# Attention scores: the low-part product on 64 rows of TensorE, with two banks in separate row groups

## The chip, the cores and the metric

The kernel runs on one core of one Trainium2 chip. The metric is the device time of one execution in microseconds (us): the median of the runs. One more execution was profiled, and its trace is what the rows below come from.

## The reference, cut to what matters

The reference is one inference step of a two-layer network. Each layer has three branches, and the third is grouped-query attention over 1024 latent tokens plus 128 context tokens. There are 8 query heads of 64 channels and 2 key/value heads, each shared by four query heads:

```python
def one_block(qi):
    sc = jnp.einsum('bqkgd,bskd->bkgqs', qi, k).astype(jnp.float32) * scale
    p = jax.nn.softmax(sc, axis=-1).astype(v.dtype)
    return jnp.einsum('bkgqs,bskd->bqkgd', p, v)
```

For a latent query, `k` has 1152 rows: the 1024 latent keys and the 128 cached ones. A second, small attention of the 128 prompt tokens over themselves runs once per layer. All inputs and outputs are float32. The other branches (a state-space scan, a Fourier mixing) and the projections that merge the three do not change.

## The kernel before

**How precision is kept.** TensorE is fed with float32 values that are split into a high part of few mantissa bits and a low remainder. A product of two values is built from high times high, high times low and low times high. A head has only 64 channels, so for the attention scores the two parts are stacked on the 128 rows of TensorE: the query tile `at_Q` holds the high part of its 64 channels in partitions 0 to 63 and the low part in 64 to 127. The key tile `at_K` has two planes: plane 0 holds the key's high part twice (in partitions 0 to 63 and again in 64 to 127), plane 1 the key's low part twice. A product of all 128 rows with plane 0 gives (high + low of the query) times the key's high part. A product with plane 1 gives (high + low of the query) times the key's low part.

**The scores.** `scores(i)` works on one item, which is one head `h` and one block `s` of 128 queries. There are 64 items per layer, so 128 in all. The 1152 keys are three columns of 384, one in each bank of the PSUM tile `pa`, which has one buffer. Each bank gets two matmuls (planes 0 and 1): six matmuls per item, each with its own weight load of the same 128 x 128 query block.

**What follows an item.** `softmax` finds the row maximum on VectorE (line 1107), takes the exponential with the row sum on ScalarE (line 143), and scales on VectorE (line 1111). `trans` turns the item's nine 128 x 128 blocks on TensorE into `pt` and `pv` banks, from which ScalarE and VectorE write the high and low parts `at_PT`. `pvm` multiplies two items' turned blocks with the values (18 matmuls), and `pv_out` adds the two halves of its result over the tile `at_t`.

**The order of the work.** `step(x)` issues `scores` of item x, then `trans` of item x - 1, then lets one group of twelve matmuls of a projection run beside it (`merges`, the blocks of `dense`), and in every second step `pvm` of the pair before. The framework draws up each engine's list at compile time, mostly in program order with ready work moved ahead, and each engine then runs its list in order. All loads and stores of these stages are issued by SyncE (SP), in one list as well.

**The tiles beside it.** `load_q(h + 1)` brings the next head's 1024 query columns at `s == 2`. The prompt's value tile `at_Vp`, the prompt's scratch `at_t` and the loads `th` of `proj_block(1, ...)`, three buffers deep, take SBUF space in the same pool.

Of the kernel before, what the change touches and what calls it, by code (L numbers as in the profile page):

```python
# [10 lines left out]
R = mybir.dt.float32r  # L11
# [8 lines left out]
SP = 128  # L20
# [5 lines left out]
NH = 8  # L26
# [76 lines left out]
class Program:  # L103
# [1007 lines left out]
        nc.vector.tensor_scalar(P[:, :n], P[:, :n], mx[:, 2:3], None, op0=OP.mult)  # L1111

    def pv_out(self, pv, n, dst):
        t = self.sb("at_t", [64, 256], bufs=1, pool=self.gp)
        self.act(t[:, :n], pv[64:128, :n])
        self.tt(dst, pv[0:64, :n], t[:, :n], OP.add)

    def attn_gen(self, l, qs_d, k_d, v_d, sgc_d, zc_d):
        nc, G = self.nc, self.gp
        KV, Q, Y, PT = {}, {}, {}, {}  # L1120

        def load_k(kv):
            KV["k", kv] = self.sb("at_K", [128, 2, 1152], R, pool=G)
            for a in range(2):
                for c in range(0, 1152, 576):
                    self.dma(KV["k", kv][:, a, c:c + 576], k_d[kv, a, :, 128 + c:704 + c])
                    yield 1

        def load_v(kv):
            KV["v", kv] = self.sb("at_V", [128, 9, 128], R, pool=G)  # L1130
            for c0, c1 in ((0, 5), (5, 9)):
                self.dma(KV["v", kv][:, c0:c1], v_d[kv, :, 1 + c0:1 + c1])
                yield 1

        def load_q(h):
            Q[h] = self.sb("at_Q", [128, SL], R, bufs=2, pool=G)
            for c in (0, 512):
                self.dma(Q[h][:, c:c + 512], qs_d[h, :, SP + c:SP + c + 512])
                yield 1

        def scores(i):
            h, s = i
            K = KV["k", h // 4]
            ps = self.ps.tile([128, 3, 512], F, name="pa", tag="pa", bufs=1)
            for j in range(3):
                for a in range(2):
                    self.mm(ps[:, j, :384], Q[h][:, 128 * s:128 + 128 * s], K[:, a, 384 * j:384 + 384 * j], a == 0, a == 1)
            P = self.sb("at_P", [128, 1152], bufs=2, pool=G)
            self.softmax(ps[:, :, :384], 1152, P)
            return P  # L1150

        def trans(i, P):
            h, s = i
            if s % 2 == 0:
                PT[h, s // 2] = [self.sb(f"at_PT{a}", [128, 9, 256], R, pool=G) for a in range(2)]
            T = PT[h, s // 2]
            c = 128 * (s % 2)
            for b in range(0, 9, 3):
                pt = self.pst("pv" if b == 6 else "pt")
                for k in range(3):  # L1160
                    self.tr(pt[:, 128 * k:128 * k + 128], P[:, 128 * (b + k):128 * (b + k) + 128])
                self.split_ps(T[0][:, b:b + 3, c:c + 128], T[1][:, b:b + 3, c:c + 128], pt[:, :384].rearrange("p (k n) -> p k n", n=128))

        def pvm(h, p):
            T = PT.pop((h, p))
            Vt = KV["v", h // 4]
            pv = self.pst("pv")
            n = 0
            for a in range(2):
                for k in range(9):  # L1170
                    self.mm(pv[:, :256], Vt[:, k], T[a][:, k], n == 0, n == 17)
                    n += 1
            self.pv_out(pv, 256, Y[h // 2][64 * (h % 2):64 * (h % 2) + 64, 256 * p:256 + 256 * p])

        def prompt():
            kp = self.sb("at_Kp", [128, 2, 2, 128], R, pool=G)
            self.dma(kp, k_d[:, :, :, 0:SP].rearrange("k a p n -> p (k a) n"))
            qp = self.sb("at_Q", [128, SL], R, bufs=2, pool=G)
            self.dma(qp.rearrange("p (h n) -> p h n", h=NH), qs_d[:, :, 0:SP].rearrange("h p n -> p h n"))
            vp = self.sb("at_Vp", [128, 2, 128], R, pool=G)  # L1180
            self.dma(vp, v_d[:, :, 0].rearrange("k p c -> p k c"))
            sg = self.sb("at_Yp", [128, 4, 128], bufs=2, pool=G)
            self.dma(sg, sgc_d[:, 0:SP].rearrange("(b p) n -> p b n", p=128))
            yield 5
            k, q = load_k(0), load_q(0)
            yield from self.some(k, 2)
            ps = self.ps.tile([128, 3, 512], F, name="pa", tag="pa", bufs=1)
            for h in range(NH):
                for a in range(2):
                    self.mm(ps[:, h // 4, 128 * (h % 4):128 * (h % 4) + 128], qp[:, 128 * h:128 * h + 128], kp[:, h // 4, a], a == 0, a == 1)  # L1190
            src = ps[:, 0:2].rearrange("p a (h n) -> p (a h) n", n=128)
            mx = self.sb("at_mp", [128, 3, NH], pool=G)
            nc.vector.tensor_reduce(out=mx[:, 0], in_=src, axis=AX.X, op=OP.max, negate=True)
            P = self.sb("at_P", [128, 1152], bufs=2, pool=G)
            P3 = P[:, 0:SL].rearrange("p (h n) -> p h n", n=128)
            for h in range(NH):
                self.act(P3[:, h], src[:, h], AF.Exp, bias=mx[:, 0, h:h + 1], accum=mx[:, 1, h:h + 1])
            nc.vector.reciprocal(mx[:, 2], mx[:, 1])
            self.tt(P3, P3, mx[:, 2][:, :, None].to_broadcast([128, NH, 128]), OP.mult)
            yield from k  # L1200
            yield from q
            yield from step(0)
            v = load_v(0)
            T = [self.sb(f"at_PT{a}", [128, 9, 256], R, pool=G).rearrange("p k n -> p (k n)") for a in range(2)]
            for q in range(2):
                pt = self.pst("pt")
                for k in range(4):
                    self.tr(pt[:, 128 * k:128 * k + 128], P3[:, 4 * q + k])
                c = slice(512 * q, 512 * q + 512)
                self.split_ps(T[0][:, c], T[1][:, c], pt)  # L1210
            yield from v
            y = self.sb("at_Yp", [128, 4, 128], bufs=2, pool=G)
            for q in range(2):
                pv = self.pst("pv")
                for a in range(2):
                    self.mm(pv, vp[:, q], T[a][:, 512 * q:512 * q + 512], a == 0, a == 1)
                for u in range(2):
                    t = self.sb("at_t", [64, 256], bufs=1, pool=G)
                    self.act(t, pv[64:128, 256 * u:256 * u + 256])
                    for e in range(2):  # L1220
                        self.tt(y[64 * e:64 * e + 64, 2 * q + u], pv[0:64, 256 * u + 128 * e:256 * u + 128 * e + 128], t[:, 128 * e:128 * e + 128], OP.add)
            self.tt(y, y, sg, OP.mult)
            self.dma(zc_d[:, 0:SP].rearrange("(b p) n -> p b n", p=128), y)

        def finish(hb):
            y = Y.pop(hb)
            for c0, c1 in ((128, 384), (384, 768), (768, 1152)):
                w = c1 - c0
                sg = self.sb("jt", [128, 384], bufs=3)
                self.dma(sg[:, :w], sgc_d[128 * hb:128 * hb + 128, c0:c1])  # L1230
                z = self.jo()
                self.tt(z[:, :w], y[:, c0 - 128:c1 - 128], sg[:, :w], OP.mult)
                self.dma(zc_d[128 * hb:128 * hb + 128, c0:c1], z[:, :w])

        items = [(h, s) for h in range(NH) for s in range(8)]
        n = len(items)
        Ps = {}

        def step(x):
            if x < n:  # L1240
                h, s = items[x]
                if x == 32:
                    self.run_all(load_k(1))
                if x == 34:
                    self.run_all(load_v(1))
                if s == 2 and h % 2 == 0:
                    Y[h // 2] = self.sb("at_Y", [128, SL], bufs=1, pool=G)
                if s == 2 and h + 1 < NH:
                    self.run_all(load_q(h + 1))
                Ps[x] = scores(items[x])  # L1250
            if 1 <= x <= n:
                trans(items[x - 1], Ps.pop(x - 1))
            yield PACE[x % 2]
            if x >= 2 and x % 2 == 0:
                h, s = items[x - 2]
                pvm(h, s // 2)
                if h % 2 == 1 and s == 6:
                    finish(h // 2)

        yield from prompt()  # L1260
        for x in range(1, n + 1):
            yield from step(x)
# [71 lines left out]
    def layer(self, l, cs):  # L1334
# [65 lines left out]
        def proj_block(n, b, th, key):  # L1400
            def ev(j, ps):
                if n == 1:
                    t = th_tile()
                    self.dma(t, rows(th["d"], b, j))
                else:
                    t = self.jt(rows(th["d"], b, j)) if "d" in th else th.pop(j)
# [256 lines left out]
```

## Time and profile before

| | |
|---|---|
| median of 3 runs | 2709.13 us (2707.88 to 2715.88) |
| the profiled execution's own time | 2707.93 us |
| its span, first to last instruction | 2706.2 us |
| granted TensorE clock, mean over the span | 0.991 of full speed |
| attention of layer 0, from its first to its last scores | about 750 to 1106 us of the span |
| attention of layer 1 | about 2070 to 2425 us |

In the profile PE is TensorE's matmuls and PEld its weight loads, which overlap matmuls. A matmul's length in a row includes its way through the array: the next one can start long before it ends. What the engine really needs per matmul is the distance from one start to the next. A weight load's row also holds more than its share of the engine. Where a matmul has to wait for its weights, the matmul's row begins with the load and is longer than usual, and the next weight load starts when that matmul really begins to stream.

### The profile page before, as it was taken

The page shows a single profiled execution, that of the slowest core. Times are in us where ns is not written, and L with a number is a line of the kernel's source. Part 1 is how long each engine was busy: PE and PEld are TensorE (multiplying, and loading weights), DVE is VectorE, ACT ScalarE, POOL GpSimd, SP SyncE. Part 2 cuts the span into 40 slices and gives each one's busy share as a digit, 9 for nine tenths or more (in the row PEclk, how much of TensorE's full clock was granted, in tenths as well). Part 3 has the DMA queues.
Part 4 walks back from the last instruction along what each step waited for, and adds up shares of the span by engine and source line. Part 5 has one row for each costly group of instructions (what it writes and reads, how often), then busy time and mean ns, then how long its engine had stood idle before and what let it go on. Part 6 is the DMA issues. An engine that isn't in the chain of part 4 may idle for free. (4 is left out here: it accounts for less than half of the span.)

```text
span 2706.2 us, 44496 instructions
## 1 busy us (share of the span) xinstructions
PE 2599.8 (96%) x16093; PEld 2502.1 (92%) x16093; DVE 1746.8 (65%) x3837; ACT 1200.5 (44%) x2754; POOL 655.4 (24%) x518
## 2 busy tenths in 40 slices
PE   6999999999999999999999999989999999999998
PEld 4999999899999899999989999989999998999997
DVE  6559964636478889847462798564654788981443
ACT  5462245741355465423345322575224556543244
POOL 1332122312321020132333312232222212101223
PEclk8999999999999999999999999999999999999999
DMA  7533233566443435535542322345645334442334
GB/s 258 154 103 102 90 105 106 168 185 199 149 139 110 143 118 154 188 96 138 172 134 86 112 86 83 119 131 166 210 142 192 104 116 155 148 125 80 92 117 145
DMA packets 459812, 366.85 MB, mean 136 GB/s; under 512 B 72816, under 2 KB 431816, under 8 KB 459592
## 3 DMA queue, kind: packets, MB, share of 16 engines
q1 hardware_dynamic: 458168, 359.68, 43.4%
q0 software_dynamic: 1424, 4.33, 0.5%
q8 instruction: 127, 2.08, 0.3%
q14 instruction: 93, 0.76, 0.1%
HBM read 243.52 MB, written 120.39 MB: 134 GB/s over the span
## 5 line engine op out<-in xcount | busy, mean ns | idle before, releaser
L169 PE MATMUL pd<-hh,whi 128*128 128x384 f32 x2496 | 854.3, 343 | 8.8 <-ACT jo L143 4.5
L169 PE MATMUL pd<-hh,wlo 128*128 128x384 f32 x2496 | 842.9, 338 | 4.7 <-POOL wlo L146 4.4
L169 PE MATMUL pd<-hl,whi 128*128 128x384 f32 x2496 | 840.2, 337 | 0.8 <-DVE hl L150 0.8
L146 POOL TENSOR_TENSOR wlo<-wst,whi 128x512 fp32r<-128x512 f32 x312 | 432.8, 1389 | 1523.1 <-ACT whi L143 1445.4
L169 PEld LDWEIGHTS pd<-hh,whi 128*128 128x128 f32 x2496 | 470.9, 189 | 14.9 <-ACT jo L143 6.1
L169 PEld LDWEIGHTS pd<-hh,wlo 128*128 128x128 f32 x2496 | 470.8, 189 | 10.0 <-POOL wlo L146 9.0
L169 PEld LDWEIGHTS pd<-hl,whi 128*128 128x128 f32 x2496 | 471.3, 189 | 2.9 <-DVE hl L150 1.9
L169 PE MATMUL pd<-A,whi 128*128 128x384 f32 x1728 | 457.7, 341 | 6.3 <-ACT jo L143 6.3
L143 ACT ACTIVATE whi<-wst 128x512 fp32r<-128x512 f32 x312 | 195.6, 630 | 291.1 <-PE pd L169 188.2
L169 PEld LDWEIGHTS pd<-A,whi 128*128 128x128 f32 x1728 | 310.9, 189 | 9.0 <-ACT jo L143 6.9
L169 PE MATMUL pd<-A,wlo 128*128 128x384 f32 x864 | 293.5, 340 | 0.0
L1107 DVE TENSOR_REDUCE at_mx<-pa 128x1 f32<-128x1152 f32 x128 | 173.2, 1353 | 16.0 <-PE pa L169 15.6
L143 ACT ACTIVATE at_PT<-pt 128x384 fp32r<-128x384 f32 (+1 forms) x260 | 114.9, 490 | 142.6 <-PE pt L174 142.2
L169 PE MATMUL pa<-at_K,at_Q 128*128 128x384 f32 x768 | 167.1, 347 | 7.8 <-ACT at_P L143 5.3
L143 ACT ACTIVATE at_P<-pa,at_mx 128x1152 f32<-128x1152 f32 x128 | 158.0, 1235 | 20.6 <-DVE at_mx L1107 19.4
L169 PEld LDWEIGHTS pd<-A,wlo 128*128 128x128 f32 x864 | 163.2, 189 | 0.1
L169 PEld LDWEIGHTS pa<-at_K,at_Q 128*128 128x128 f32 x768 | 128.2, 188 | 28.2 <-ACT at_P L143 25.2
L169 PE MATMUL pt<-qkW,hh 128*128 128x384 f32 x576 | 151.9, 345 | 0.5 <-DVE qk_xn L146 0.5
L169 PE MATMUL pv<-at_PT,at_V 128*128 128x256 f32 x1152 | 148.8, 283 | 0.0
L143 ACT ACTIVATE jo<-pd 128x384 f32<-128x384 f32 x120 | 58.1, 485 | 199.9 <-PE pd L169 113.0
L169 PEld LDWEIGHTS pv<-at_PT,at_V 128*128 128x128 f32 x1152 | 144.7, 191 | 0.8
L146 DVE TENSOR_TENSOR at_PT<-pt,at_PT 128x384 fp32r<-128x384 f32 (+1 forms) x260 | 133.1, 550 | 9.3 <-ACT at_PT L143 8.6
(297 smaller groups left out, 3719.5 us busy)
## 6 DMA issues: line engine op xcount, KB each, us to landing
aw<-in_ada_w_dram SPq DMA_DIRECT2D x48, 512.0 KB, 4.5
wst<-in_merge_w_dram SPq DMA_DIRECT2D x96, 256.0 KB, 2.9
wst<-in_w_in_dram SPq DMA_DIRECT2D x80, 256.0 KB, 3.0
td<-jo SPq DMA_DIRECT2D x96, 192.0 KB, 1.9
jt<-td SPq DMA_DIRECT2D x96, 192.0 KB, 2.7
wst<-in_w_out_dram SPq DMA_DIRECT2D x64, 256.0 KB, 2.8
sgd<-jo SPq DMA_DIRECT2D x72, 192.0 KB, 1.8
jt<-sgd SPq DMA_DIRECT2D x64, 192.0 KB, 3.0
```

The lines of the kernel that those rows point to most:

```text
L143: return self.nc.scalar.activation(out, in_, func, **kw)
L146: return (e or self.nc.vector).tensor_tensor(out=out, in0=a, in1=b, op=op)
L169: return self.nc.tensor.matmul(out, w, x, start=first, stop=last, **kw)
L1107: nc.vector.tensor_reduce(out=mx[:, 0:1], in_=src, axis=AX.XY if m3 else AX.X, op=OP.max, negate=True)
```

## The change

Plane 0 is multiplied as before: three matmuls of 128 rows. The product with plane 1 now uses 64 rows, the query's high part alone; the low-times-low term is no longer computed. Banks 0 and 2 take it from partitions 0 to 63 (`tile_position=(0, 0)`). Bank 1 takes it from partitions 64 to 127 (`tile_position=(64, 0)`), where a new tile `at_Q2` holds a second copy of the query's high part. `at_Q2` has 512 columns and two buffers; its halves are loaded by `load_q2` at `s == 5` for the next head's first half, at `s == 1` for the second half, and once ahead of the first item. To make room, the prompt's value tile shares the buffer of `at_t`, the prompt's scratch comes from the `jo` tiles, and the `th` loads of `proj_block(1, ...)` go from three buffers to two.

```diff
     def pv_out(self, pv, n, dst):
-        t = self.sb("at_t", [64, 256], bufs=1, pool=self.gp)
+        t = self.sb("at_t", [128, 256], bufs=1, pool=self.gp)[0:64]
...
+        def load_q2(h, i):
+            Q[h, i] = self.sb("at_Q2", [128, 512], R, bufs=2, pool=G)
+            self.dma(Q[h, i][64:128], qs_d[h, 0:64, SP + 512 * i:SP + 512 * i + 512])
+
         def scores(i):
...
             for j in range(3):
-                for a in range(2):
-                    self.mm(ps[:, j, :384], Q[h][:, 128 * s:128 + 128 * s], K[:, a, 384 * j:384 + 384 * j], a == 0, a == 1)
+                self.mm(ps[:, j, :384], Q[h][:, 128 * s:128 + 128 * s], K[:, 0, 384 * j:384 + 384 * j], True, False)
+            Q2, c = Q[h, s // 4], 128 * (s % 4)
+            lo = (Q[h][0:64, 128 * s:128 + 128 * s], K[0:64, 1], (0, 0))
+            hi = (Q2[64:128, c:c + 128], K[64:128, 1], (64, 0))
+            for j, (w, k, pos) in enumerate((lo, hi, lo)):
+                self.mm(ps[:, j, :384], w, k[:, 384 * j:384 + 384 * j], False, True, tile_position=pos)
...
-            vp = self.sb("at_Vp", [128, 2, 128], R, pool=G)
+            vp = self.sb("at_t", [128, 256], pool=G).rearrange("p (k c) -> p k c", k=2).bitcast(R)
...
+            load_q2(0, 0)
             yield from step(0)
...
-                    t = self.sb("at_t", [64, 256], bufs=1, pool=G)
+                    t = self.sb("jo", [128, 384], bufs=3)[0:64, 0:256]
...
+                if x > 0 and s == 5 and h + 1 < NH:
+                    load_q2(h + 1, 0)
+                if x > 0 and s == 1:
+                    load_q2(h, 1)
                 Ps[x] = scores(items[x])
...
-                    t = th_tile()
+                    t = th_tile(bufs=2)
```

## Rows read from the trace of the kernel before

**Rows 1.** The page's busy times: us, share of the span, instructions.
```profile
PE 2599.8 (96%) x16093; PEld 2502.1 (92%) x16093; DVE 1746.8 (65%) x3837; ACT 1200.5 (44%) x2754; POOL 655.4 (24%) x518
```

**Rows 2.** Busy time per engine in three stretches: dense matmuls alone, then both attentions.
```profile
250.00:300.00 50.00, 50.00 (x290) 50.00 (x289) 47.18 (x167) 10.51 (x20) 10.42 (x8) 1.00 0.28 90
...
749.00:1145.00 396.00, 385.75 (x2548) 367.29 (x2547) 329.96 (x556) 212.54 (x434) 65.13 (x51) 1.00 0.45 139
2045.00:2440.00 395.00, 386.63 (x2557) 369.20 (x2556) 313.49 (x529) 211.51 (x441) 61.74 (x52) 1.00 0.45 139
```

**Rows 3.** Chain of waits within 2060 to 2440 us, by engine and line.
```profile
by line: PE pd L169 32.9%; PE pv L169 16.2%; PE pa L169 15.9%; PE pt L174 9.6%; PE pv L174 4.5%; ACT at_P L143 3.1%; DVE at_P L1111 2.6%; issue 2.4%; ACT at_PT L143 2.0%; DMA jo<-zbd 1.9%; POOL A L146 1.4%; DMA jt<-zbd 1.0%; DMA jt<-zad 0.8
```

**Rows 4.** Timeline around one item's scores: start, us, engine, operation, idle before.
```profile
905.22 1.36 DVE L1107 TENSOR_REDUCE at_mx<-pa 128x1 f32<-128x1152 f32 x1 [0.16 <-PE pa L169]
906.67 1.24 ACT L143 ACTIVATE at_P<-pa,at_mx 128x1152 f32<-128x1152 f32 x1
908.05 0.99 PEld L169 LDWEIGHTS pa<-at_K,at_Q 128*128 128x128 f32 x6 [0.27 <-ACT at_P L143]
908.05 1.33 PE L169 MATMUL pa<-at_K,at_Q 128*128 128x384 f32 x6
```

**Rows 5.** Timeline of TensorE around transposes of 32 rows.
```profile
75.62 0.33 PE L169 MATMUL pd<-hh,whi 128*128 128x384 f32 x1
75.62 0.19 PEld L169 LDWEIGHTS pd<-hl,whi 128*128 128x128 f32 x1
75.80 0.34 PE L169 MATMUL pd<-hl,whi 128*128 128x384 f32 x1
76.06 0.14 PEld L174 LDWEIGHTS pv<-ident,ss_ld 32*128 32x128 f32 x1 [0.25 <-issue]
76.24 0.19 PEld L169 LDWEIGHTS pd<-hh,wlo 128*128 128x128 f32 x1
76.35 0.19 PEld L169 LDWEIGHTS pd<-hh,whi 128*128 128x128 f32 x1
77.41 0.34 PE L169 MATMUL pd<-hh,whi 128*128 128x384 f32 x1
77.68 0.19 PEld L174 LDWEIGHTS pv<-ident,ss_st 32*128 32x128 f32 x1 [0.25 <-ACT sst_lim L143]
77.91 0.19 PEld L169 LDWEIGHTS pd<-hl,whi 128*128 128x128 f32 x1
```

**Rows 6.** Timeline of TensorE around two groups at positions of 32 columns.
```profile
494.55 0.34 PE L169 MATMUL pd<-hh,wlo 128*128 128x384 f32 x1
494.82 1.02 PE L169 MATMUL pt<-ss_CK,ss_B 128*32 128x240 f32 x16
630.65 0.34 PE L169 MATMUL pd<-A,wlo 128*128 128x384 f32 x1
630.92 0.25 PE L169 MATMUL pt<-aR,fold 128*32 128x8 f32 x8
```

**Rows 7.** Timeline of weight loads around a transpose of 32 columns without a position.
```profile
466.14 0.09 PEld L174 LDWEIGHTS pv<-ident,ss_fin 128*32 128x32 f32 x1 [1.49 <-ACT qk_qo L143]
466.17 0.19 PEld L169 LDWEIGHTS pd<-hh,wlo 128*128 128x128 f32 x1
```

**Rows 8.** The tile `at_Q`: its loads, and their us from issue to landing.
```profile
L128 SPq DMA_DIRECT2D at_Q<-qsd x34: 319/423/779, 718.2 to 2336.5; - x34
...
DMA to landing us min/median/max: 2.7/3.2/6.8
```

**Rows 9.** SP's timeline as the first head's query loads are issued.
```profile
741.81 0.79 SPq L128 DMA_DIRECT2D at_Q<-qsd  x2
```

**Rows 10.** VectorE's readings of `th` at their closest, and the us its loads take.
```profile
1036.24 0.54 DVE L150 SCALAR_TENSOR_TENSOR jo<-th,pd 128x384 f32<-128x384 f32 x1
1042.78 0.56 DVE L150 SCALAR_TENSOR_TENSOR jo<-th,pd 128x384 f32<-128x384 f32 x1
...
DMA to landing us min/median/max: 2.2/2.6/6.6
```

## The prediction

> **What bounds the kernel now.** I read the page's busy times first. TensorE is busy 96% of the span and every other engine is at 65% or less [rows 1]. The table by stretch shows the same for the two attentions: about 386 of 395 us on PE, 330 and 313 on VectorE [rows 2]. The chain of waits over the second attention says how much of that is binding: the five PE entries add up to 79%, the scores (`pa`) alone to 15.9% [rows 3]. Of 380 us that is 60 us. The scores themselves need 64 x 6 x 0.173 = 66 us, because a 384-column matmul costs 0.173 us from start to start (50 us for 290 of them, [rows 2]). So nine tenths of the scores' time lies on the path that sets the end. The rest is covered by VectorE and ScalarE.
>
> The timeline of one item shows why a longer `scores` can't hide well [rows 4]. The first weight load at 908.05 waited 0.27 us for the exponential of the item before, which frees `pa`. After the scores, VectorE's reduction takes 1.36 us and the exponential 1.24 us, and then `pa` is free again. So in such a step the loop is scores, reduction, exponential, scores; in the other steps PE's own list is full. Both contain the scores, so what is added to or taken from them moves the next item by as much.
>
> **The change, part by part: the six matmuls.** The number of matmuls and weight loads stays at six per item, and the columns stay at 384. What changes is that three of them use 64 rows, and that two of these three may run beside each other. I count from the start of the last 128-row matmul of the item (t = 0) to the point where the next full-height matmul really streams.
>
> Before: three more matmuls and the next one, 4 x 0.173 = 0.69 us.
>
> After, from the nearest rows. No matmul of 64 rows stands in the trace, but transposes of 32 rows between full-height matmuls do [rows 5], and groups at 32-column positions [rows 6].
> - Way in: the full-height matmul starts at 75.80, the 32-row weight load only at 76.06; the second case is 77.41 to 77.68, and at 32-column positions it is 494.55 to 494.82 and 630.65 to 630.92. So it is 0.27 us each time. A usual load starts as the matmul before it begins. The 0.27 is 0.16 of streaming (384 columns at 2.4 GHz) and 0.11 in which the array empties. Load at t = 0.27.
> - The load itself is now exposed: in the row of 76.24, a load with nothing ahead of it, the next load starts 0.11 us later, and that is when the matmul begins to stream. Bank 0 streams at 0.38.
> - Bank 1 sits in the other row group with its own weights. At column positions sixteen matmuls of 240 columns fit into 1.02 us with their ends [rows 6]; one after another they would stream 1.6 us at 2.4 GHz, so groups do run beside each other there. I take the same for row groups: bank 1 costs nothing.
> - Bank 2 needs rows 0 to 63 again: one spacing later, t = 0.55, and it streams until 0.71.
> - Way out: the 32-row load at 77.68 is followed by the full-height load at 77.91 [rows 5]. Of these 0.23 us, 0.11 is the load and 0.01 the 32 columns; about 0.10 is the array emptying again. Full-height load at 0.81, and its matmul streams at 0.92.
>
> So the item costs 0.92 - 0.69 = 0.23 us more (0.22 with unrounded starts; I take 0.22), although one of six matmuls became free. 128 items x 0.22 = 28 us; of this nine tenths are on the path: 25 us.
>
> Bounds: if 64 rows needed no emptying, only the free matmul would be left, -0.17 us per item and -22 us. A transpose of 32 columns without a position shows that not every small shape pays: the full-height load follows 0.03 us after its own load [rows 7]. If the row groups ran one after the other, 0.22 + 0.17 = 0.39 us per item, +50 us. I take the middle value, since all four cases in rows 5 and 6 agree to 0.01 us and two of them are of fewer rows.
>
> Two rules of the Trainium skill bear on this. First, its page "TensorE: Matmul & The Clock Gate" (Part 3, "What overlaps and what doesn't") says that a weight load runs under a matmul in flight only if it goes to another row group. The trace disagrees for full height: a load of 128 rows and a matmul of 128 rows both begin at 75.62 [rows 5], and the spacing of 0.173 us [rows 2] has no room for 0.16 of streaming and a bare load. By the rule bank 2's load would wait for bank 0's end and add 0.09 us per item, another 11 us. I go by the trace. Second, "TensorEngine Tiling" (Key Properties) says that changing the tiling mode, not just the tile, empties the engine. It is the rule against this change: by it 64 rows pay like 32. Rows 5 and 6 show the wait for 32; no row here shows it for 64.
>
> **The loads of the second copy.** `load_q2` adds 1 + 7 + 8 = 16 DMAs per layer, 128 KB each. The nearest rows are those of `at_Q`, 0.3 to 0.8 us of SP each and 2.7 to 6.8 us to landing [rows 8]. All but the first of a layer are issued three items before their use (some 17 us, with 64 items in the 356 us of the table), so they are hidden by the items between. The first of layer 0 follows the `at_Q` loads issued at 741.81 to 742.60 [rows 9], so it lands between 745.3 and 749.7, and the scores start at 750. If that cover were gone, it would cost up to 4 us once. Each load waits in SP's list for a buffer last read two items earlier. Behind it stand stores of `td`, loads of `jt`, `th` and weights, which wait for the current item's results anyway. A gain is excluded, since nothing is removed. I take 0, and 0 to 4 us for the range.
>
> **The rearranged tiles.** With two `th` buffers, a load can start when the reading two before it ends. At their closest the one ends at 1036.78 and the load's own reading comes at 1042.78, 6.0 us later, against 2.6 us to landing in the middle and 6.6 at worst [rows 10]: 0, at most one or two stalls of 0.6 us. The value tile in `at_t` is read before `pv_out` first writes there, and the prompt's four scratch copies per layer wait at most for a `jo` store: 0, at most 2 us in all.
>
> **The sum.** 2707.9 (the profiled execution) + 25 = 2733. The median before is 1.2 us above that execution, so I forecast 2734 us, 0.9% slower.
>
> **The rivals.**
> - *Faster: 64 rows cost no emptying.* The place is the same six matmuls, and the price -0.17 x 128 = -22 us: 2687. For it: rows 7, and that no row has 64 rows. Against it: 32-row shapes pay in each of the rows 5. It decides from an exposed wait under 0.17 us per item, both ways together; the rows make it 0.39 (0.27 + 0.11 - 0.17 in, 0.10 + 0.11 - 0.03 out).
> - *No change: the addition is hidden.* In some stretches VectorE is the later one: it is busy 83% of the first attention [rows 2], and a fifth of the chain is not PE [rows 3]. If only a quarter of 28 us came through, it would be +7 us: 2716. Against it: the chain has 15.9% on `pa`.
> - *Slower still: bank 2's load is bare (0.11 less the usual gap of 0.01 to 0.02, so 0.09 x 128 = 11 us), or the row groups don't overlap (0.17 x 128 = 22 us).* 2745 to 2756. For it: no row has two row groups. Against it: column groups overlap in rows 6.
> - That the change doesn't do what it says would be seen in that the 64-row matmuls are not in the list; the diff leaves no room for it.
>
> **How the numbers follow.** A measurement of this kernel tells about 0.3% (8 us) from no change. Forecast 0.70, with its own range of 2724 to 2745; faster 0.09; hidden 0.07; slower still 0.14. So faster 0.09, same 0.07, slower 0.84. The range of 2714 to 2753 leaves out the faster case, part of the hidden one and the upper third of the last: under 2 in 10.
>
> **What would show it.** In the changed trace three matmuls per item have 64 rows. If I am right, the first 64-row load starts 0.27 us after the last 128-row matmul, banks 0 and 1 start within a few hundredths, bank 2 about 0.17 later, and the next 128-row load 0.1 us after its streaming ends. A 64-row load that starts with the matmul before it would prove the forecast wrong and give the faster case. Starts of banks 0 and 1 that lie 0.17 apart would give the slower one. Scores whose spacing grew by 0.22 us without the total growing would show it hidden.

## The result and the profile after

The changed kernel takes 2727.09 us (median of 4 runs, 2725.92 to 2731.72) against 2708.56 for the kernel before (4 runs beside it): a ratio of 1.0069 [1.0054, 1.0083], 18.5 us slower where 25 were forecast. Its profiled execution took 2726.75 us with a span of 2725.0; the span before was 2706.2, so the two spans differ by 18.8 us.

The page's busy times come first, against [rows 1]: the counts of instructions are the same on every engine, PE is busy 24 us longer, and PEld 32 us less.

```profile
PE 2624.2 (96%) x16093; PEld 2470.5 (91%) x16093; DVE 1748.1 (64%) x3837; ACT 1198.6 (44%) x2754; POOL 652.7 (24%) x518
```

The table by stretch says where. The columns are the stretch and its length, then the busy time of PE, PEld, VectorE, ScalarE and GpSimd, the granted clock, DMA share and GB/s. Each stretch is an attention, as in [rows 2], taken a little longer because the attention ends later. The clock is 1.00 in both kernels, so no part of the 18.5 us is a clock.

```profile
749.00:1151.00 402.00, 394.46 (x2527) 348.23 (x2525) 328.75 (x552) 211.93 (x434) 65.16 (x51) 1.00 0.46 140
2055.00:2460.00 405.00, 397.17 (x2552) 351.58 (x2551) 314.47 (x528) 210.46 (x440) 61.21 (x52) 1.00 0.46 140
```

From the first score matmul of a layer to its last, the timeline gives 355.5 and 354.4 us before, and 363.5 and 365.1 after. These are +8.0 and +10.7, together 18.7 us: all of the difference of the spans. Outside the attentions single stretches moved by up to 3 us in either direction, as they do between the two profiled executions of the changed kernel (this one and the later one on another chip).

In the chain of waits over the second attention (2070 to 2460 us), the scores' share on PE has grown from 15.9% [rows 3] to 17.6%: some 60 us became 69.

```profile
by line: PE pd L169 35.1%; PE pa L169 17.6%; PE pv L169 17.3%; PE pt L174 11.4%; PE pv L174 4.9%; DVE at_P L1111 2.8%; ACT at_P L143 2.1%; ACT at_PT L143 1.0%; DMA at_K<-kd 0.9%; DMA jo<-zad 0.9%; DVE jo L150 0.8%; issue 0.8%; DMA jt<-td 0.
```

Now one item from close by, as [rows 4] showed it before. This is the timeline of TensorE in the changed kernel: start, us, engine, operation, tile, shape, count, and in brackets the idle time before it. The view merges neighbours, so rows that overlap were read in different narrow stretches.

```profile
906.29 0.71 PE L169 MATMUL pa<-at_K,at_Q 128*128 128x384 f32 x3
906.56 0.19 PEld L169 LDWEIGHTS pa<-at_K,at_Q 64*128 64x128 f32 x2 [0.25 <-issue]
906.67 0.19 PEld L169 LDWEIGHTS pa<-at_K,at_Q 64*128 64x128 f32 x1
906.56 0.44 PE L169 MATMUL pa<-at_K,at_Q 64*128 64x384 f32 x2
906.84 0.34 PE L169 MATMUL pa<-at_K,at_Q 64*128 64x384 f32 x1
907.10 0.14 PEld L174 LDWEIGHTS pt<-ident,at_P 128*128 128x128 f32 x1 [0.25 <-DVE at_Y L146]
```

The first row holds the last 128-row matmul, which starts at 906.29, merged with the first two of 64 rows. From there the reader can follow the prediction's steps:

- The first 64-row load starts at 906.56, 0.27 us later, as forecast. "Issue" as the releaser says that no other engine held it.
- Two loads of 0.19 us each fill only 906.56 to 906.75. So they began together: 906.559 and 906.563, and the rows of their matmuls 3 ns apart. Banks 0 and 1 do stream beside each other.
- Bank 2's load starts at 906.67, just as bank 0, in the same rows, begins to stream. It is not bare, and its matmul starts at 906.84, 0.17 after 906.67. The Trainium skill's page "TensorE: Matmul & The Clock Gate" (Part 3, "What overlaps and what doesn't") allows a load under a matmul only in another row group. For 64 rows the trace disagrees too.
- The next load of full height starts at 907.10, 0.26 after bank 2's start. By the prediction's estimate (384 columns at 2.4 GHz) 0.16 of it is streaming, which leaves 0.10 of emptying. That a change of tiling mode empties the engine is what "TensorEngine Tiling (Array Packing)" (Key Properties) of the Trainium skill says, and for 64 rows the trace agrees.

What differs is the last term, the bare load on the way out. Here a transpose follows, and its load is 0.14 us long, not 0.19; the next load begins 0.054 later, at 907.16. Where a matmul of the projection follows, the load is one of 0.19, and the next begins 0.11 later:

```profile
910.91 0.29 PEld L169 LDWEIGHTS pa<-at_K,at_Q 64*128 64x128 f32 x3 [0.25 <-issue]
911.46 0.19 PEld L169 LDWEIGHTS pd<-A,whi 128*128 128x128 f32 x1 [0.25 <-issue]
911.56 0.19 PEld L169 LDWEIGHTS pd<-A,wlo 128*128 128x128 f32 x1
```

I measured from the start of an item's third 128-row matmul to the point where the next full-height matmul really streams, over all items. Before, this is 0.71 us. After, it is 0.866 where a transpose follows (74 items, +0.154) and 0.918 where a projection matmul follows (48 items, +0.207). That makes 74 x 0.154 + 48 x 0.207 = 21 us. In the other six items the list that was fixed at compile time put other work between the first and the other two matmuls of 64 rows, so that TensorE changes its height twice: 18 matmuls of `pv` in four of them, five transposes and a projection matmul in two. One of the four, in the timeline of TensorE:

```profile
993.87 0.70 PE L169 MATMUL pa<-at_K,at_Q 128*128 128x384 f32 x2
994.13 0.43 PE L169 MATMUL pa<-at_K,at_Q 64*128 64x384 f32 x1
994.50 2.42 PE L169 MATMUL pv<-at_PT,at_V 128*128 128x256 f32 x18
996.84 0.44 PE L169 MATMUL pa<-at_K,at_Q 64*128 64x384 f32 x2
```

In these four the way from the first score matmul to the next full-height matmul that streams is 0.56 us longer than in the same items before, where the `pv` matmuls stood at the same place; the six together are 2.4 us longer. So about 23 us were added on TensorE (PE's busy time within the two attentions rose by 22), and 18.7 came through: four fifths.

Where the last fifth went can be read from the steps (from one item's first score matmul to the next item's). In 24 of the 126 steps the time is within 0.06 us of before; in most of the others it grew by 0.15 to 0.2 us, the full price. In one of the 24, TensorE waited for VectorE's scaling of the probabilities both before (scores at 896.27) and after (scores at 898.27):

```profile
898.87 0.30 PE L174 MATMUL pt<-ident,at_P 128*128 128x128 f32 x1 [0.74 <-DVE at_P L1111]
900.86 0.30 PE L174 MATMUL pt<-ident,at_P 128*128 128x128 f32 x1 [0.53 <-DVE at_P L1111]
```

The transposes begin 2.60 us after the scores in the one and 2.59 in the other: the wait became 0.21 shorter and took the addition in. Two more of the 24 show the same.

### The profile page after: what moved, and what is told of

Read it like the earlier page. It is cut to its first block, busy times and chain, and to the rows that moved or that the text cites. A ratio compares the mean times of both kernels' runs of the same rounds, so it can differ in the third digit from the quotient of the medians.

```text
span 2725.0 us, 44551 instructions
## 1 busy us (share of the span) xinstructions
PE 2624.2 (96%) x16093; PEld 2470.5 (91%) x16093; DVE 1748.1 (64%) x3837; ACT 1198.6 (44%) x2754; POOL 652.7 (24%) x518
## 5 line engine op out<-in xcount | busy, mean ns | idle before, releaser
L169 PEld LDWEIGHTS pd<-A,whi 128*128 128x128 f32 x1728 | 310.6, 189 | 15.9 <-ACT jo L143 7.1
L169 PE MATMUL pa<-at_K,at_Q 128*128 128x384 f32 (+1 forms) x768 | 169.4, 380 | 4.9 <-ACT at_P L143 3.9
L169 PEld LDWEIGHTS pa<-at_K,at_Q 128*128 128x128 f32 (+1 forms) x768 | 100.6, 186 | 55.7 <-issue 31.2
```

Source lines behind the costliest of these rows:

```text
L169: return self.nc.tensor.matmul(out, w, x, start=first, stop=last, **kw)
```

## The experiments

Theory: the changes of height cost what the rows say (0.27 + 0.11 in, 0.10 and a bare load out, less one matmul that runs beside another), and nothing else in the change costs anything. Rivals: the extra loads and rearranged tiles cost part of it; the row groups do not really help; or the time comes from how ScalarE's list stands to TensorE's. "Step" below is the time from one item's first score matmul to the next item's. In the quiet stretches an odd step (no `pv` product) takes 4.086 us before and 4.240 after, an even one 6.740 and 6.940. All times are medians, with the kernel before run beside.

**The low product on 64 rows, all in one row group, no second copy.**

```diff
-            for j, (w, k, pos) in enumerate((lo, hi, lo)):
-                self.mm(ps[:, j, :384], w, k[:, 384 * j:384 + 384 * j], False, True, tile_position=pos)
+            for j in range(3):
+                self.mm(ps[:, j, :384], Q[h][0:64, ...], K[0:64, 1, 384 * j:384 + 384 * j], False, True, tile_position=(0, 0))
```

> Before with the low-part product on 64 rows, but all three banks in row group (0, 0), so without the second copy and with the buffers of before. Theory, two changes of height per item are paid and the group at (64, 0) gives back one matmul of 0.172 us: the item costs 0.17 us more than in the change, 22 us over 128 items, of which 0.85 reaches the end: 2745 us (2740 to 2750). Rival, the two row groups do not run beside each other in effect: the same as the change, 2727. Rival, the loss is the second copy's loads: 2708.

Measured: 2743.05 us against 2711.19, ratio 1.0114 [1.0094, 1.0134], +31.9 us, inside what was expected. Steps grew by 0.171 and 0.155 us over those of the changed kernel. The loads of one item, in the timeline of this kernel:

```profile
909.21 0.18 PEld L169 LDWEIGHTS pa<-at_K,at_Q 64*128 64x128 f32 x1 [0.25 <-issue]
909.31 0.36 PEld L169 LDWEIGHTS pa<-at_K,at_Q 64*128 64x128 f32 x2
909.92 0.14 PEld L174 LDWEIGHTS pt<-ident,at_P 128*128 128x128 f32 x1 [0.25 <-DVE at_Y L146]
```

The second load starts 0.11 us after the first (909.205 and 909.314), under the first matmul, and the third one spacing later (0.36 for two loads of 0.18). The load of full height follows 0.71 us after the first, against 0.54 in the changed kernel (906.56 to 907.10). So the second row group saves just one matmul, 0.17 us per item, and the height alone costs 0.33 to 0.36 per step (odd and even steps against those of before).

**The kernel before, with one small matmul of 64 rows and 64 columns behind the six.**

```diff
+            self.mm(ps[:, 0, 384:448], Q[h][0:64, 128 * s:128 + 128 * s], K[0:64, 1, 0:64], True, True, tile_position=(0, 0))
```

> Before with one more matmul per item, after the six: 64 rows, 64 columns, into a part of the bank that nobody reads. No work is saved, so it prices one pair of height changes. Theory: 0.11 of emptying and 0.11 of bare load on the way in, 0.03 of streaming, 0.10 of emptying and 0.05 to 0.11 of bare load on the way out, 0.39 to 0.44 us per item; 128 x 0.41 = 52 us, of which 0.85 reaches the end: 2753 us (2746 to 2762). Rival, a change of height is cheap and the 64-row matmuls themselves are slow: only one more load, 0.11 us per item, 2720 to 2723.

Measured: 2760.73 us against 2711.19, ratio 1.018 [1.0158, 1.0202], +49.5 us, near the upper end of what the theory gave. One of its items, in the timeline of weight loads:

```profile
930.80 0.18 PEld L169 LDWEIGHTS pa<-at_K,at_Q 64*128 64x128 f32 x1 [0.26 <-issue]
931.03 0.19 PEld L169 LDWEIGHTS pd<-A,wlo 128*128 128x128 f32 x1
931.13 0.19 PEld L169 LDWEIGHTS pd<-A,whi 128*128 128x128 f32 x1
```

The last 128-row matmul started at 930.536 and the next one streams at 931.135: 0.60 us where the usual spacing is 0.17. A matmul that itself streams some 0.03 us (64 of the 384 columns that take 0.16) cost 0.43. Where a transpose follows (84 items) it cost 0.37. Over 128 items that is about 50 us, and 49.5 reached the end. The reduction starts 0.23 us later here, since it waits for the small matmul too, but it still ends 0.25 us ahead of the exponential, so it adds nothing. This is the price of a change of height by itself.

**Five matmuls of 128 rows: bank 1's low product left out.**

```diff
-                for a in range(2):
+                for a in range(1 if j == 1 else 2):
```

> Before without the low-part product of bank 1 (left out of the computation), all at 128 rows: five matmuls per item. It is the gain that the change would have without changes of height. Theory, scores lie on the path for 0.85 to 0.9 of their time: 128 x 0.173 x 0.87 = 19 us less, 2689 us (2685 to 2693). Rival, the loop is held by the reduction, the copies and the exponential, and TensorE's time is mostly covered: 2702 to 2708.

Measured: 2696.45 us against 2711.19, ratio 0.9942 [0.9923, 0.996], -14.7 us. Both answers missed: of the 22 us that went from TensorE two thirds passed (by the interval, 11 to 21 us). Odd steps are 0.184 us shorter where the list stayed as it was, but the attentions as a whole only by 6.1 and 4.5 us, since the list of TensorE came out differently elsewhere. So "nine tenths" is not a property of the loop: here about two thirds of what was taken away reached the end, and nearly all of what the small matmul added.

**The loads and tiles alone.** The first attempt was the changed kernel with the six matmuls of before; its copy is loaded and not read.

```diff
             for j in range(3):
+                for a in range(2):
+                    self.mm(ps[:, j, :384], Q[h][:, ...], K[:, a, ...], a == 0, a == 1)
```

> All of the change but the matmuls: the loads of the second copy, the shared value tile, the jo scratch and the two th buffers stay, the scores are the six 128-row matmuls of before (nothing reads the second copy). Theory, the whole loss is the change of height on TensorE: same as before, 2708.5 us within 4. Rival, the loads or the rearranged tiles cost a good part of the 18.5 us: 2715 to 2727.

Measured: 2716.53 us (10 runs) against 2711.19, ratio 1.0019 [1.0006, 1.0032]: +5 us, which looks like a cost of the loads. The steps say otherwise. The profiled execution, 11.9 us longer than that of before, has 10.2 of it in the first three steps of each layer (+2.27 and +2.10 us in layer 0; +0.76, +3.87 and +1.20 in layer 1). Most later steps agree with before within 0.02, and the rest of them add 1 us in sum. SP's timeline as layer 0's attention begins:

```profile
740.58 6.00 SPq L128 DMA_DIRECT2D at_Q<-qsd  x6
...
749.74 0.45 SPq L128 DMA_DIRECT2D at_Q<-qsd  x1
750.24 0.58 SPq L128 DMA_DIRECT2D zbd<-jo  x1
750.87 0.43 SPq L128 DMA_DIRECT2D jt<-sgd  x1
751.40 0.45 SPq L128 DMA_DIRECT2D at_Q<-qsd  x1
...
754.61 1.15 SPq L128 DMA_DIRECT2D at_Q<-qsd  x2
```

and the first copy of the prompt's part on ScalarE, which waits for a store of `jo`:

```profile
759.86 0.38 ACT L143 ACTIVATE jo<-pv 64x256 f32<-64x256 f32 x1 [4.22 <-DMA zbd<-jo]
```

With nobody reading the copies, nothing holds their loads back, and the list has many of them here, in front of the stores of `jo` that the prompt's part waits for. The changed kernel does not do this: its first two steps differ by +0.26 and +0.03 us. The run therefore measured an effect of its own. The second attempt lets the copy be read: all 128 rows of it (256 KB, twice the change's bytes), by bank 1's two full-height matmuls.

```diff
+            self.dma(Q[h, i], qs_d[h, :, SP + 512 * i:SP + 512 * i + 512])
...
+                q = Q2[:, c:c + 128] if j == 1 else Q[h][:, 128 * s:128 + 128 * s]
                 for a in range(2):
-                    self.mm(ps[:, j, :384], Q[h][:, ...], K[:, a, ...], a == 0, a == 1)
+                    self.mm(ps[:, j, :384], q, K[:, a, ...], a == 0, a == 1)
```

> The change's loads and tiles again, this time with the second copy in use: all 128 rows of it are loaded (256 KB instead of 128), and the middle bank's two 128-row matmuls read their weights from it; the scores are six 128-row matmuls, as before, and compute what they did before. Theory, the 4 to 6 us of the run with all but the matmuls came from copies that nothing read and that were therefore pulled together into the prompt's stretch: same as before within 3 us, and steps of 4.09 and 6.74 us again from the first item on. Rival, the loads, the jo scratch or the two th buffers cost 5 us by themselves: 5 us over before, and the first steps are late again.

Measured: 2709.96 us (10 runs) against 2708.59, ratio 1.0002 [0.9991, 1.0013]. The steps are 4.086 and 6.740 again. The loads, the two `th` buffers and the moved tiles together cost nothing that can be measured (by the interval, -2.4 to +3.5 us). In the profiles one step of layer 1 is 1.2 us longer than before in this kernel and in the changed one, and TensorE waits there for VectorE's scaling; so up to 1 us of the 18.7 may be theirs.

**What holds the next item in an odd step.** The prediction called the loop scores, reduction, exponential. ScalarE's rows of the item at 905.95, in the changed kernel, with the reduction ahead of them:

```profile
907.21 1.36 DVE L1107 TENSOR_REDUCE at_mx<-pa 128x1 f32<-128x1152 f32 x1 [0.17 <-PE pa L169]
907.69 0.87 ACT L143 ACTIVATE at_PT<-pt 128x384 fp32r<-128x384 f32 x2 [1.09 <-PE pt L174]
908.44 0.50 ACT L143 ACTIVATE at_PT<-pv 128x384 fp32r<-128x384 f32 x1
908.81 1.24 ACT L143 ACTIVATE at_P<-pa,at_mx 128x1152 f32<-128x1152 f32 x1
```

and in the kernel before, where the scores start at 903.96 (its reduction and exponential are in [rows 4]):

```profile
905.54 0.88 ACT L143 ACTIVATE at_PT<-pt 128x384 fp32r<-128x384 f32 x2 [0.94 <-PE pt L174]
906.30 0.50 ACT L143 ACTIVATE at_PT<-pv 128x384 fp32r<-128x384 f32 x1
```

Counted from the scores' start, the reduction begins 1.252 us later before and 1.260 after: the change hardly delays it. The exponential begins 2.710 and 2.861 later. In both kernels it stands 0.37 us behind the start of the third copy of the turned blocks, and that copy waits for the transposes, which stand behind the scores on TensorE. The reduction ends 0.10 us ahead of the exponential before and 0.24 after, where 0.03 is the least in either trace. So the loop is TensorE, copies, exponential, and the reduction has slack, but little in the kernel before: 0.07 us, against 0.21 after. To test this, the third copy was issued behind the exponential, in the steps without a `pv` product, in both kernels.

```diff
-        self.act(dst, src, AF.Exp, bias=mx[:, 0:1], accum=mx[:, 1:2])
+        self.exp = self.act(dst, src, AF.Exp, bias=mx[:, 0:1], accum=mx[:, 1:2])
...
-                self.split_ps(T[0][:, b:b + 3, c:c + 128], ...)
+                with (self.tc.issue_after(self.exp.ins) if b == 6 and s % 2 == 0 and s < 7 else ExitStack()):
+                    self.split_ps(T[0][:, b:b + 3, c:c + 128], ...)
```

On the kernel before:

> Before, with ScalarE's exponential of an item put ahead of the third copy of turned blocks in the steps without the product with the values. It tests what frees the scores' bank. If ScalarE's list holds it (three copies, then the exponential), the exponential starts 0.07 us earlier in some 55 of these steps: 2 to 4 us less than before. If the reduction holds it, as the prediction had it: no change. The list of TensorE shifts a little with it, which may cost or give 2 us either way.

Measured: 2707.95 us (12 runs) against 2708.59, ratio 0.9998 [0.9987, 1.0009]. Undisturbed odd steps fell from 4.086 to 4.010 us, but other steps took it back, and the attentions came out 1.4 and 4.6 us longer. The expected 2 to 4 us are not there, so the total decides nothing; that the copies held these steps is shown by the 0.076 us that they lost, just about the slack.

On the changed kernel:

> The changed kernel with the same shift of the exponential. There the transposes and so the three copies come 0.15 us later, and the reduction only 0.01: if ScalarE's list holds the loop, the exponential can start up to 0.24 us earlier in some 55 steps, but TensorE's own list then ends the step (0.27 us of waiting before, less 0.15 to 0.2 of the change), so 0.1 to 0.2 us per step come back: 6 to 11 us less than the changed kernel, 2716 to 2721. If the reduction holds it: 2727.

Measured: 2717.29 us (10 runs) against 2708.59, ratio 1.0037 [1.0027, 1.0048]; odd steps fell from 4.240 to 4.123 us. That is inside what was expected, but it was compared with the changed kernel across two chips. So both were run again on one:

> The changed kernel again, on one chip with the one that follows. The changed kernel with the exponential ahead took 8.7 us more than before and the changed kernel 18.5, but not side by side, and in the profiles only 2 us of that lie in the attentions (17 against 19 us longer than before). Theory, the way of the two kernels outside the attentions differs by chance of the transfers: within 4 us of each other, both 12 to 19 us over before. Rival, the shift of the exponential gives back half of the loss: 18 us over before here, 9 there.

> The changed kernel with the exponential ahead of the third copy, beside the changed kernel on the same chip. Theory: within 4 us of the changed kernel. Rival: 8 to 10 us less than the changed kernel, and the attentions shorter by that.

Measured: the changed kernel 2727.67 us against 2707.37, ratio 1.0074 [1.0061, 1.0087]; with the exponential first 2717.31, ratio 1.0044 [1.003, 1.0058]. The 10 us are real, and my expectation of less than 4 was wrong. ScalarE's rows in the latter kernel:

```profile
907.27 0.87 ACT L143 ACTIVATE at_PT<-pt 128x384 fp32r<-128x384 f32 x2 [0.76 <-PE pt L174]
908.39 1.23 ACT L143 ACTIVATE at_P<-pa,at_mx 128x1152 f32<-128x1152 f32 x1 [0.25 <-DVE at_mx L1107]
909.60 0.48 ACT L143 ACTIVATE at_PT<-pv 128x384 fp32r<-128x384 f32 x1
```

The exponential now follows the reduction, and the copy comes behind it: the wait moved as intended. But in the two profiles the attentions account for only 1.6 and 2.1 us of them, 3.7 together. Another 5 lie in the stretch right after the first attention, where nothing was edited: from the end of the last score matmul to the start of TensorE's 7079th matmul, the same one in both lists, it takes 87.6 us and 82.3 (86.5 and 82.6 in the earlier profiles of the same two kernels). Other stretches came out up to 3 us longer, so that the two profiled executions differ by 4.7 us in all, and the changed kernel's was the fastest of its five. What makes that stretch shorter, and where the rest of the 10 us lies, stays open. On the kernel before, the same edit gained nothing, so none of the kernels that compute the whole change beats it.

## Why the prediction was right

- **Way in, both row groups, bank 2's load.** Each came out to 0.01 us: 0.27, starts 3 ns apart, 0.17. The run in one row group shows the second group's worth (0.17 per item), and the run with the small matmul shows the price of the height without the rest (0.37 to 0.43).
- **Emptying on the way out.** 0.10 us as forecast.
- **The bare load on the way out was the mis-sized term.** I used 0.11 for all 128 items, from the load at 76.24 of [rows 5]. For the 74 items that a transpose follows it is 0.054. [rows 5] had the sign of it: of its two transposes one has a load of 0.19 and is followed after 0.23 us, the other a load of 0.14 and is followed after 0.18, and I used only the first. The way before was also set at 0.69 where it measures 0.71. The two take 4 and 2.5 us off, so that these terms sum to 21 us and not 28.
- **Not foreseen:** the six items whose 64-row matmuls are split by other work, 2.4 us in all. Nothing ties the six matmuls together in the list.
- **Loads and tiles at nothing:** right within 3 us or so, by the run that reads the copy.
- **Nine tenths on the path:** 18.7 of about 23 us came through, so four fifths, since 24 steps passed nothing: in the three followed above TensorE had a wait to spare, for the others that is not shown. The sum (28 against 23) and the share (0.9 against 0.8) were both too high, and that is the way from the forecast 25 to the measured 18.5. The share of the chain is no constant: the runs passed anything from about two thirds (five matmuls, where the lists were rearranged) to nearly all (the small matmul).
- **The loop was named wrongly in a detail.** Scores are in it, so the sum did not suffer, but through the transposes and ScalarE's copies, not through the reduction. For the reduction the way in (0.38 until bank 0 streams) is nearly paid by the free matmul, which is why it moved by 0.008 us only; the way out is what delays the copies. In the kernel before the two ways are within 0.07 us of each other, so [rows 4] alone could hardly tell them apart.
- **The rivals.** "No emptying" fell with 906.29 to 906.56, "row groups don't overlap" and "bank 2's load is bare" with the loads at 906.56 and 906.67, "hidden" with the +18.7 us of the attentions.

## What to carry to other kernels

Price a change of TensorE's row height before using row groups: here 0.27 + 0.11 us going in and 0.10 plus a bare load going out, less the usual spacing, 0.33 to 0.43 us per pair of changes in these runs. One freed matmul of 0.17 us does not pay for that. As an estimate from these numbers, which no run here tests, two freed matmuls of 384 columns per pair come out about even and three pay, if the 64-row matmuls stay together in the list. And a run in which a load is made but not read can mislead about the load's cost: here, without a reader, it moved to another place.

## What was not expected of the hardware

- The load of the transposes of `at_P` holds TensorE for 0.054 us, one ahead of these matmuls for 0.107; the recorded lengths, 0.14 and 0.19, differ by the same 0.05. Why is not shown, and one transpose of [rows 5] has the longer load.
- Two loads into different row groups start 4 ns apart (906.559 and 906.563); a few hundredths of a us were forecast.
- Taking 22 us from TensorE gave 14.7 us, while adding some 50 cost 49.5.
